# The down projection's split weights: low parts on the vector engine, buffers shared with the activations

## The chip, the cores and the metric

One core of one Trainium2 chip. A core has five engines that run their own queues of instructions: TensorE (PE in the profile: matmuls into PSUM; PEld: its loads of the stationary operand), the vector engine (DVE), the scalar engine (ACT), GpSimd (POOL) and SyncE (SP), which here issues all DMA transfers. The metric is the device time of one execution in microseconds (us).

## The reference

One layer of a decoder trunk on an input of 1024 rows (tokens) of 1024 float32 values: a mixer (recurrent heads and a causal convolution), a residual sum with a norm, and a gated feed-forward part with a second residual sum. The part that matters here is the feed-forward part:

```python
D_MODEL, SEQ, D_FF = 1024, 1024, 2816
def _conv_ffn(h, ffn_up, ffn_conv_w, ffn_conv_b, ffn_down):
    hid = h @ ffn_up                                     # 1024 x 5632
    hid = _causal_dwconv(hid, ffn_conv_w, ffn_conv_b)    # width 3
    gate, up = hid[..., :D_FF], hid[..., D_FF:]
    return (jax.nn.gelu(gate, approximate=True) * up) @ ffn_down   # the down projection
...
x = x + _rms_norm(f, norm_post_ffn)                      # f: its result
```

All of it is float32.

## The kernel before

**Split operands.** A float32 matmul is made of three matmuls on a faster format (float32r): an operand is split into a high part (a cast, on ACT) and a low part (the operand minus its high part), and high x high, high x low and low x high are added up in PSUM. `split` (L153) issues both: the cast on ACT, and the subtraction on POOL or DVE. `weight` (L158) loads a weight tile of 128x512 (256 KB) with a DMA on SP into a raw buffer (tag `wr`, three of them) and splits it into `wh` and `wl` (two buffers of each). Its low part is made on POOL unless the weight is a held one. Activations are split too, with the low part on DVE, into pairs of tiles called `a`, from the pool `h1p`, which has 16 tiles (8 pairs).

**The down projection** (`ffn_down`, L947) multiplies a 1024 x 2816 matrix by a 2816 x 1024 one in quarters, with seven products instead of eight (the Strassen-Winograd scheme). The rows fall in two halves, 0 and 1, and the inner dimension in two halves of 11 tiles of 128 (`HT` = 11): `A11`, `A12` are lists of 11 activation tiles of half 0, `A21`, `A22` of half 1. The weights' combinations (`T(n)`) were added up earlier, by `weight_sums`, and lie in DRAM (`sums`). The other three products read `ffn_down` itself (`B(r, c)`). The activations' combinations are made during the products:

- product 1 (`A11`) and 3 (`A12`) add up in the four banks `X`, product 2 (`A11 - A21`, tiles `s`) and 4 (`A22`) in the banks `Y`, product 5 (`A22`) in `X`, product 6 (`A11`) in `Y`, product 7 (`A12`) in `X`;
- while product 4 runs, `after4` adds `A21` to `A22`; with product 5, `after5` turns `A11` into `A22 - A11`; with product 6, `after6` turns `A12` into `A12 - A11`. These are 33 additions of 128x512 on DVE (line 959 in the profile; the tiles are called `act` or `row` by the pool that they lie in). Each may run as soon as its operands are ready, also ahead of its product.

`product` (L965) goes through the 11 tiles j: it splits the activation tile, calls `then(j)` (the additions), loads and splits the weight, and issues 12 matmuls, three for each of four row tiles t. At the end it calls `after(t)` for each row tile.

**Held weights.** Seven weights of product 7 are loaded and split ahead, during products 5 and 6 (`hold`): raw in `f2p` (six buffers, which also serve the pieces of the input in the last step), high and low part in `hp`, the 16 tiles in which `A21` and five tiles of `A22` lie until they are used up. Their low parts are made on DVE. The matmuls of held weights come last and in the order of t, so that the four row tiles end one after the other and the norm and output of one go on beside the matmuls of the next (`last`, `second`, `norm`, `ffn_out`).

**Order.** The instructions' order on each engine is set before the run by a scheduler that works with priorities and estimated times: `high_priority` puts a block ahead of everything without it, and within that the program's order decides among what is ready. On the chip each engine works its queue in that order and waits where an operand or a buffer isn't ready.

Of the kernel before, what the change touches and what calls it, by code (L numbers as in the profile page):

```python
# [12 lines left out]
F32 = mybir.dt.float32  # L13
F32R = mybir.dt.float32r
# [7 lines left out]
P = 128  # L22
# [16 lines left out]
HT = FT // 2  # L39
# [2 lines left out]
LN_EPS = 1e-5  # L42
GN_EPS = 64e-5

HELD = 7
DECAY = math.exp(-0.5)


# [46 lines left out]
class Trunk:  # L95
    def __init__(self, ctx, tc, a):
        self.ctx, self.tc, self.nc, self.a = ctx, tc, tc.nc, a
        self.at = dict(PRIO)
        self.n = 0


    def nm(self, s):
# [28 lines left out]
    def after(self, i, first):  # L131

        self.tc.add_manual_dep(
            i.ins, first.ins.name,
            mybir.DependencyInfo(mybir.DependencyClass.NoSync, mybir.DependencyReason.DATA),
            reason="the bank's first matmul clears it")
# [18 lines left out]
        eng = self.nc.gpsimd if pool else self.nc.vector  # L155
        return self.nc.scalar.copy(hi, src), eng.tensor_tensor(lo, src, hi.bitcast(F32), ALU.subtract)  # L156

    def weight(self, src, shape, home=None, held=False):  # L158

        with self.tc.high_priority():  # L160
            raw = (self.f2p.tile(shape, F32, tag="f2", name=self.nm("wr")) if held else
                   self.wp.tile(shape, F32, tag="wr", bufs=3, name=self.nm("wr")))
            self.nc.sync.dma_start(raw, src)
            if held:
                hi, lo = (self.hp.tile(shape, F32R, tag="h", name=self.nm("w")) for _ in range(2))
            elif home:
                hi, lo = (home[0].tile(shape, F32R, tag=t, bufs=BUFS[t], name=self.nm("wm")) for t in home[1:])
            else:
                hi, lo = (self.wp.tile(shape, F32R, tag=t, bufs=2, name=self.nm(t)) for t in ("wh", "wl"))
            self.low = self.split(hi, lo, raw, not held)[1]  # L170
        return hi, lo


# [773 lines left out]
    def ffn_down(self, acts):  # L947
        nc = self.nc
        first = self.tc.high_priority
        A11, A12, A21, A22 = acts[0][:HT], acts[0][HT:], acts[1][:HT], acts[1][HT:]  # L950
        B = lambda r, c: lambda j: self.a["ffn_down"][c, r * HT + j]
        T = lambda n: lambda j: self.sums[n - 1, j]
        X = [self.bank() for _ in range(4)]
        Y = [self.bank(("pb", "pn")[t // 2]) for t in range(4)]
        halves = lambda: [row[:, c * 512:(c + 1) * 512] for row in (self.row("nrow", 4) for _ in range(2)) for c in range(2)]
        four = lambda: [self.tp.tile([P, 512], F32, tag="tp", name=self.nm("c")) for _ in range(4)]

        def tt(out, a, b, op=ALU.add):
            nc.vector.tensor_tensor(out, a, b, op)  # L959
            return out  # L960

        def s3(j):
            return tt(self.f2p.tile([P, HALF], F32, tag="f2", name=self.nm("s3")), A11[j], A21[j], ALU.subtract)

        def product(banks, src, wt, start, after, then=lambda j: None, held=(), soon=True):  # L965
            ops, n = [], HT - len(held)
            for j in range(HT):
                with first():
                    hi, lo = self.pair("a", self.h1p)
                    self.split(hi, lo, src(j))  # L970
                    then(j)
                wh, wl = self.weight(wt(j), [P, 512]) if j < n else held[j - n]
                op = (hi, wh), (hi, wl), (lo, wh)
                if j >= n:
                    ops.append(op)
                else:
                    for t in range(4):
                        mms(banks[t], t, op, start and j == 0, j == HT - 1)

            ins = []  # L980
            for t in range(4):
                for i, op in enumerate(ops):
                    ins += mms(banks[t], t, op, False, i == len(held) - 1)
                with first() if soon else ExitStack():
                    after(t)
            self.chain(ins)

        def mms(ps, t, op, start, stop):
            return [self.mm(ps, a[:, t * P:(t + 1) * P], w, start=start and i == 0, stop=stop and i == 2, skip=True)
                    for i, (a, w) in enumerate(op)]  # L990

        def norm(h, t, c, f, src, junk):
            nc.scalar.activation(junk, src, AF.Square, accum_out=self.fss[:, 4 * h + t, c:c + 1])  # L993
            tt(f, src, self.post_ffn[:, c * 512:(c + 1) * 512], ALU.mult)

        s1, s7 = halves(), halves()
        product(X, lambda j: A11[j], B(0, 0), True, lambda t: nc.scalar.copy(s1[t], X[t]))
        product(Y, s3, T(3), True, lambda t: nc.scalar.copy(s7[t], Y[t]))
        c11 = four()
        product(X, lambda j: A12[j], B(1, 0), False, lambda t: norm(  # L1000
            0, t, 0, c11[t], X[t], self.f2p.tile([P, 512], F32, tag="f2", name=self.nm("junk"))))
        c21 = four()
        late = []

        def hold(j, every=2):

            if j % every == 1 and len(late) < HELD:
                late.append(self.weight(B(1, 1)(HT - HELD + len(late)), [P, 512], held=True))


        def after4(j):
            tt(A22[j], A21[j], A22[j])

        def after5(j):
            hold(j, 3)
            tt(A11[j], A22[j], A11[j], ALU.subtract)

        def after6(j):
            hold(j)
            tt(A12[j], A12[j], A11[j], ALU.subtract)  # L1020

        product(Y, lambda j: A22[j], T(4), False, lambda t: tt(c21[t], s1[t], Y[t]), after4)
        product(X, lambda j: A22[j], T(1), True, lambda t: tt(s7[t], s7[t], X[t]), after5)

        def second(t):
            tt(c21[t], c21[t], Y[t])
            tt(s1[t], s1[t], Y[t])
            norm(1, t, 0, c21[t], c21[t], Y[t])
            tt(s7[t], s7[t], s1[t])
            norm(1, t, 1, s7[t], s7[t], Y[t])  # L1030
            self.ffn_out(4 + t, (c21[t], s7[t]))

        def last(t):
            tt(s1[t], s1[t], X[t])
            norm(0, t, 1, s1[t], s1[t], X[t])
            self.ffn_out(t, (c11[t], s1[t]))

        product(Y, lambda j: A11[j], T(2), True, second, after6, soon=False)
        product(X, lambda j: A12[j], B(1, 1), False, last, held=late)
# [258 lines left out]
```

## Time and profile before

| | |
|---|---|
| median of 3 runs | 1340.19 us (1337.7 to 1342.9) |
| the profiled execution | 1338.02 us, of it 1336.2 us from the first to the last instruction (the span) |
| mean granted TensorE clock | 0.982 |
| busy share of the span | PE 95%, DVE 64%, ACT 51%, POOL 46% |
| matmuls of the down projection | from 1089.3 us to 1325.6 us of the span |

A row of the groups gives line, engine, operation, output<-inputs, shapes and count, then busy time in us and the mean of one in ns, then the idle time of the engine just ahead of these instructions and what ended it. A row of the waits gives the waiting engine with its tile and line, the one it waited for, the us in all, the number of times, and the longest. A row of the timeline gives the start in us, the length in us, the engine and the instruction, xN for N merged ones, and in brackets the idle time before it.

### The profile page before, as it was taken

The page shows a single profiled execution, that of the slowest core. Times are in us where ns is not written, and L with a number is a line of the kernel's source. Part 1 is how long each engine was busy: PE and PEld are TensorE (multiplying, and loading weights), DVE is VectorE, ACT ScalarE, POOL GpSimd, SP SyncE. Part 2 cuts the span into 40 slices and gives each one's busy share as a digit, 9 for nine tenths or more (in the row PEclk, how much of TensorE's full clock was granted, in tenths as well). Part 3 has the DMA queues.
Part 4 walks back from the last instruction along what each step waited for, and adds up shares of the span by engine and source line. Part 5 has one row for each costly group of instructions (what it writes and reads, how often), then busy time and mean ns, then how long its engine had stood idle before and what let it go on. Part 6 is the DMA issues. An engine that isn't in the chain of part 4 may idle for free. (4 is left out here: it accounts for less than half of the span.)

```text
span 1336.2 us, 22956 instructions
## 1 busy us (share of the span) xinstructions
PE 1266.3 (95%) x8580; PEld 1019.7 (76%) x8580; DVE 860.7 (64%) x1450; ACT 679.6 (51%) x1354; POOL 618.8 (46%) x522
## 2 busy tenths in 40 slices
PE   6999989999899989999999999999999989996996
PEld 5767767777678767787798788888888878875885
DVE  5377998997799989885521463455555365295347
ACT  6563654657755765656543564333333344443451
POOL 4343423354333322444462467667676454445441
PEclk9999979999999999999999999999999999997998
DMA  6322211222123441222355655665654323343325
GB/s 213 79 77 62 72 40 49 52 69 56 50 66 104 149 144 50 64 72 79 103 162 172 234 197 179 199 191 178 197 177 139 95 79 95 95 122 123 95 80 204
DMA packets 85647, 155.79 MB, mean 117 GB/s; under 512 B 9280, under 2 KB 15808, under 8 KB 85536
## 3 DMA queue, kind: packets, MB, share of 16 engines
q1 hardware_dynamic: 85536, 154.33, 38.1%
q8 instruction: 67, 1.10, 0.4%
q14 instruction: 44, 0.36, 0.1%
HBM read 129.13 MB, written 25.17 MB: 115 GB/s over the span
## 5 line engine op out<-in xcount | busy, mean ns | idle before, releaser
L156 POOL TENSOR_TENSOR wl<-wr,wh 128x512 fp32r<-128x512 f32 x350 | 474.9, 1358 | 548.9 <-ACT wh L156 522.2
L129 PE MATMUL pb<-f,wh 128*128 128x512 f32 x1408 | 442.3, 395 | 3.2 <-ACT pb L771 1.8
L156 ACT CAST wh<-wr 128x512 fp32r<-128x512 f32 x350 | 215.1, 615 | 326.5 <-PE pb L129 167.4
L129 PEld LDWEIGHTS pb<-f,wh 128*128 128x128 f32 x1408 | 263.7, 188 | 61.9 <-ACT pb L771 2.0
L129 PE MATMUL pb<-f,wl 128*128 128x512 f32 x704 | 280.1, 398 | 2.0 <-POOL wl L156 2.0
L129 PE MATMUL pb<-h,wh 128*128 128x512 f32 (+3 forms) x720 | 229.8, 399 | 2.5 <-ACT wh L156 1.9
L877 DVE SCALAR_TENSOR_TENSOR acc<-pb,params,acc 128x511 f32<-128x511 f32 (+1 forms) x128 | 95.5, 746 | 183.8 <-ACT acc L872 123.9
L399 DVE SCALAR_TENSOR_TENSOR pc<-c,params,pc 128x512 f32<-128x512 f32 x232 | 174.2, 751 | 4.6 <-ACT pc L396 0.5
L129 PEld LDWEIGHTS pb<-f,wl 128*128 128x128 f32 x704 | 132.6, 188 | 35.7 <-POOL wl L156 5.4
L129 PEld LDWEIGHTS pb<-h,wh 128*128 128x128 f32 (+2 forms) x720 | 132.3, 189 | 34.4 <-ACT wh L156 4.3
L129 PE MATMUL pb<-h,wl 128*128 128x512 f32 (+3 forms) x360 | 146.7, 408 | 3.0 <-POOL wl L156 2.8
L129 PE MATMUL pb<-wh,a 128*128 128x512 f32 x428 | 141.9, 400 | 3.4 <-ACT wh L156 3.4
L129 PEld LDWEIGHTS pb<-wh,a 128*128 128x128 f32 x428 | 81.4, 191 | 23.8 <-ACT wh L156 4.3
L129 PE MATMUL pb<-wl,a 128*128 128x512 f32 x214 | 86.7, 405 | 11.3 <-POOL wl L156 11.3
L129 PEld LDWEIGHTS pb<-h,wl 128*128 128x128 f32 (+2 forms) x360 | 68.1, 189 | 22.3 <-POOL wl L156 5.8
L156 DVE TENSOR_TENSOR a<-act,a 128x512 fp32r<-128x512 f32 x50 | 37.3, 746 | 66.1 <-ACT a L156 66.1
L156 ACT CAST a<-act 128x512 fp32r<-128x512 f32 x50 | 31.0, 621 | 71.7 <-PE pn L129 47.5
L129 PEld LDWEIGHTS pb<-wl,a 128*128 128x128 f32 x214 | 41.1, 192 | 23.1 <-POOL wl L156 13.3
L877 DVE SCALAR_TENSOR_TENSOR pt<-pb,params,pt 128x511 f32<-128x511 f32 (+1 forms) x48 | 35.8, 746 | 33.7 <-ACT ecarry L874 33.1
L917 POOL TENSOR_TENSOR b<-b,b 128x512 f32<-128x512 f32 x44 | 57.0, 1295 | 0.9
L872 ACT ACTIVATE acc<-pb,params 128x512 f32<-128x512 f32 x64 | 49.5, 774 | 1.8 <-PE pb L129 1.8
L129 PE MATMUL pn<-wh,a 128*128 128x512 f32 x132 | 47.8, 403 | 0.0
(297 smaller groups left out, 1928.3 us busy)
## 6 DMA issues: line engine op xcount, KB each, us to landing
wr<-ffn_up SPq DMA_DIRECT2D x176, 256.0 KB, 2.7
wr<-w_in SPq DMA_DIRECT2D x80, 256.0 KB, 2.6
b<-ffn_down SPq DMA_DIRECT2D x44, 256.0 KB, 4.0
sums<-b SPq DMA_DIRECT2D x44, 256.0 KB, 2.4
wr<-sums SPq DMA_DIRECT2D x44, 256.0 KB, 2.6
wr<-ffn_down SPq DMA_DIRECT2D x33, 256.0 KB, 2.6
wr<-w_out SPq DMA_DIRECT2D x32, 256.0 KB, 2.7
mixd<-t SPq DMA_DIRECT2D x16, 256.0 KB, 3.2
```

The source lines that it names most:

```text
L129: return self.nc.tensor.matmul(out, lhsT, rhs, start=start, stop=stop, skip_group_check=skip)
L156: return self.nc.scalar.copy(hi, src), eng.tensor_tensor(lo, src, hi.bitcast(F32), ALU.subtract)
L399: nc.vector.scalar_tensor_tensor(out, c[:, j:j + HALF], w(j), acc, ALU.mult, ALU.add)
L872: nc.scalar.activation(acc, ps, AF.Identity, scale=w(2), bias=self.par("fb", ch))
L877: nc.vector.scalar_tensor_tensor(acc[:, o:], ps[:, :HALF - o], w(j), acc[:, o:], ALU.mult, ALU.add)
L917: sub = lambda o, x, y, op=ALU.subtract: nc.gpsimd.tensor_tensor(o, x, y, op)
```

## The change

In the down projection, the low part of every weight is made on DVE (`low_pool` turns False as `ffn_down` begins; the earlier stages keep POOL). Weights of odd j that aren't held take their high and low tiles from the 16 tiles of `h1p`, in turn with the activations' pairs; those of even j keep `wh` and `wl`. Both load into the three raw buffers. Five weights of product 7 are held instead of seven, so six of its weights are streamed.

```diff
-HELD = 7
+HELD = 5
...
+        self.low_pool = True
...
-    def weight(self, src, shape, home=None, held=False):
+    def weight(self, src, shape, home=None, held=None):
 
         with self.tc.high_priority():
-            raw = (self.f2p.tile(shape, F32, tag="f2", name=self.nm("wr")) if held else
+            raw = (self.f2p.tile(shape, F32, tag="f2", name=self.nm("wr")) if held is self.hp else
                    self.wp.tile(shape, F32, tag="wr", bufs=3, name=self.nm("wr")))
             self.nc.sync.dma_start(raw, src)
             if held:
-                hi, lo = (self.hp.tile(shape, F32R, tag="h", name=self.nm("w")) for _ in range(2))
+                hi, lo = self.pair("w", held)
             elif home:
...
-            self.low = self.split(hi, lo, raw, not held)[1]
+            self.low = self.split(hi, lo, raw, self.low_pool)[1]
...
     def ffn_down(self, acts):
         nc = self.nc
         first = self.tc.high_priority
+        self.low_pool = False
...
-                wh, wl = self.weight(wt(j), [P, 512]) if j < n else held[j - n]
+                wh, wl = self.weight(wt(j), [P, 512], held=self.h1p if j % 2 else None) if j < n else held[j - n]
...
-                late.append(self.weight(B(1, 1)(HT - HELD + len(late)), [P, 512], held=True))
+                late.append(self.weight(B(1, 1)(HT - HELD + len(late)), [P, 512], held=self.hp))
```

## The prediction

> **What bounds the kernel now.** I read the page first, then the busy times by stretch over the last 280 us (the down projection), then what TensorE (PE) waited for there, and last the instructions in order of time at the two places where it waited.
>
> ```profile
> span 1336.2 us, 22956 instructions
> PE 1266.3 (95%) x8580; PEld 1019.7 (76%) x8580; DVE 860.7 (64%) x1450; ACT 679.6 (51%) x1354; POOL 618.8 (46%) x522
> ...
> L156 POOL TENSOR_TENSOR wl<-wr,wh 128x512 fp32r<-128x512 f32 x350 | 474.9, 1358 | 548.9 <-ACT wh L156 522.2
> ...
> L156 ACT CAST wh<-wr 128x512 fp32r<-128x512 f32 x350 | 215.1, 615 | 326.5 <-PE pb L129 167.4
> ```
>
> PE is busy 95% of the span, so what a change off PE can win is PE's holes. The down projection's columns by stretch are length, then busy time and count for PE, PEld, DVE, ACT and POOL, then the granted PE clock:
>
> ```profile
> 1085.00:1100.00 15.00, 11.51 (x44) 8.91 (x43) 12.40 (x19) 7.71 (x15) 10.42 (x4) 0.89 0.20 57
> ...
> 1125.00:1156.00 31.00, 31.00 (x134) 24.95 (x134) 7.63 (x11) 14.70 (x28) 14.21 (x11) 1.00 0.33 94
> 1156.00:1187.00 31.00, 31.00 (x135) 24.95 (x134) 21.62 (x22) 14.71 (x29) 15.10 (x11) 1.00 0.33 94
> 1187.00:1220.00 33.00, 21.74 (x78) 15.68 (x77) 27.37 (x41) 12.52 (x25) 16.91 (x7) 0.79 0.48 151
> ...
> 1233.00:1264.00 31.00, 31.00 (x134) 24.98 (x133) 11.35 (x17) 12.76 (x23) 14.21 (x11) 1.00 0.35 94
> ```
>
> PE is full in three of the five stretches. It has 3.5 us of hole in 1085 to 1100 and 11.3 us in 1187 to 1220, and the clock is lower in just these two. How much that is in all comes from the matmuls of the seven products, from the first to the last:
>
> ```profile
> 1089.33 1.09 PE L129 MATMUL pb<-wh,a 128*128 128x512 f32 x4
> ...
> L129 PE MATMUL pb<-wh,a 128*128 128x512 f32 x428 | 141.9, 400 | 3.4 <-ACT wh L156 3.4
> L129 PE MATMUL pb<-wl,a 128*128 128x512 f32 x214 | 86.7, 405 | 11.3 <-POOL wl L156 11.3
> L129 PE MATMUL pn<-wh,a 128*128 128x512 f32 x132 | 47.8, 403 | 0.0
> L129 PE MATMUL pn<-wl,a 128*128 128x512 f32 x66 | 26.6, 403 | 0.0
> ...
> 1305.82 19.76 PE L129 MATMUL pb<-w,a 128*128 128x512 f32 x84
> ```
>
> 428 + 214 + 132 + 66 + 84 = 924 matmuls (7 products x 11 weights x 12). The last 84 run without a hole: (19.76 - 0.40) / 83 = 0.2333 us each, and 2.80 us a weight. 924 of them need 215.6 us. They took 1325.58 - 1089.33 - 0.16 (the last one's overlap) = 236.1 us. So **20.5 us** are lost: 5.1 at the first place (15 - 11.51 = 3.5 idle, and 0.11 x 15 = 1.6 by the clock), and the other 15.4 around the second.
>
> Who is late there, first place and then second, with POOL's instructions at both:
>
> ```profile
> PE pb L129 <- POOL wl L156: 3.5, 1, 3.5
> ...
> PE pb L129 <- POOL wl L156: 7.8, 3, 7.5
> ACT w L156 <- DVE act L959: 6.0, 1, 6.0
> PE pb L129 <- ACT wh L156: 3.4, 2, 3.0
> ...
> 1087.23 8.39 POOL L156 TENSOR_TENSOR wl<-wr,wh 128x512 fp32r<-128x512 f32 x2 [1.50 <-PE pb L129]
> ...
> 1193.51 1.29 POOL L156 TENSOR_TENSOR wl<-wr,wh 128x512 fp32r<-128x512 f32 x1 [2.60 <-ACT wh L156]
> ...
> 1205.64 10.21 POOL L156 TENSOR_TENSOR wl<-wr,wh 128x512 fp32r<-128x512 f32 x2 [5.93 <-ACT wh L156]
> ```
>
> A weight's low part takes POOL 1.29 us; two together took 8.39 and 10.21 us, 5.8 and 7.6 too many. What DVE did meanwhile, from 1205.6 to 1213.4:
>
> ```profile
> L959 DVE TENSOR_TENSOR act<-act,act 128x512 f32<-128x512 f32 x8 | 5.2, 685 | 0.0
> L156 DVE TENSOR_TENSOR a<-act,a 128x512 fp32r<-128x512 f32 x3 | 2.1, 685 | 0.0
> L156 DVE TENSOR_TENSOR w<-wr,w 128x512 fp32r<-128x512 f32 x2 | 1.4, 686 | 0.0
> L959 DVE TENSOR_TENSOR act<-act,row 128x512 f32<-128x512 f32 x1 | 0.7, 684 | 0.0
> ```
>
> Fourteen instructions with two operands in SBUF each, at full pace (0.69 us), idle 0.0: while DVE runs such a chain, POOL's instruction stands still. The other 3.4 us come through ACT: its cast of a held weight waited 6.0 us for DVE, and PE's next weight was queued behind it. The reverse shows too, over 1156 to 1220:
>
> ```profile
> L959 DVE TENSOR_TENSOR act<-act,act 128x512 f32<-128x512 f32 x17 | 14.6, 871 | 0.1
> L156 DVE TENSOR_TENSOR a<-act,a 128x512 fp32r<-128x512 f32 x18 | 13.4, 747 | 15.7 <-ACT a L156 15.7
> L959 DVE TENSOR_TENSOR row<-act,row 128x512 f32<-128x512 f32 x8 | 9.5, 1186 | 0.2
> L959 DVE TENSOR_TENSOR act<-act,row 128x512 f32<-128x512 f32 x8 | 7.4, 920 | 0.0
> L156 DVE TENSOR_TENSOR w<-wr,w 128x512 fp32r<-128x512 f32 x7 | 5.9, 850 | 0.3 <-ACT w L156 0.3
> L959 DVE TENSOR_TENSOR c<-pb,post_ffn 128x512 f32<-128x512 f32 x4 | 2.6, 677 | 0.0
> ```
>
> 62 instructions, 53.4 us; at 0.685 they would be 42.5. So about 10.9 us of DVE time went to instructions that POOL held up.
>
> **The change, part by part.**
>
> *Low parts to DVE.* 70 streamed weights change engine, 1.29 us on POOL for 0.69 on DVE. The waits of PE for POOL (3.5 and 7.8) go, and with them the lowered clock behind them. DVE pays 11 x 0.69 = 7.6 us a product. Where PE is full it has room: 7.6 + 7.6 = 15.2 of 31 us in 1125 to 1156, 11.4 + 7.6 = 19.0 of 31 in 1233 to 1264. In 1156 to 1187 it is 21.6 + 7.6 = 29.2 of 31, before what the end of the sharing gives back. Over 1156 to 1220 POOL made 11 + 7 = 18 low parts: + 12.3 us on DVE, - 10.9 us for the sharing, - 1.4 us for two held weights fewer, so + 0.0. DVE's load at its fullest place stays as it is. The additions of the later products that fill it may run late there: they are wanted one or two products on, 31 us each.
>
> [...]
>
> *Odd weights in the activations' 16 buffers.* Before, a weight's buffer came free when PE had done the weight two before it: one weight's time, 2.80 us, for a cast (0.62) and POOL's 1.29. Now even weights have the two pairs for themselves, so the buffer is free three weights ahead (8.4 us) for 0.62 + 0.69. The eight shared pairs serve 1.5 pairs a weight instead of 1: 5.3 weights ahead, 14.9 us, where it was 8. Each split needs 1.3 us of that. Cost zero; were the ring's order bad, rival 3 prices it. The transfers stay 77 x 256 KB and in the program's order; the three raw buffers come free after a low part as before, 0.6 us earlier each.
>
> *Five held weights, not seven.* Two weights of the last product go from the quarter-by-quarter part to the streamed part. PE's 924 matmuls are the same. In the crowded place two casts, two low parts and two transfers fewer stand in line: good for ACT's 3.4 us wait, but that wait hangs on the buffers that DVE's additions free. I bound what is left of the second place from 0 to 3.4 us, beside the case in which all of it stays (rival 1), and take 1.5, near half of the largest wait, 3.0, since DVE's load there is unchanged while POOL no longer upsets the order.
>
> *The tail.* After product six DVE works through sums and squares to the first output:
>
> ```profile
> 1293.42 0.69 DVE L959 TENSOR_TENSOR c<-c,pb 128x512 f32<-128x512 f32 x1 [0.28 <-PE pb L129]
> ...
> L959 DVE TENSOR_TENSOR nrow<-nrow,nrow 128x512 f32<-128x512 f32 x4 | 3.8, 958 | 0.0
> L959 DVE TENSOR_TENSOR c<-c,post_ffn 128x512 f32<-128x512 f32 x4 | 3.7, 954 | 0.0
> ...
> 1311.13 0.75 DVE L944 SCALAR_TENSOR_TENSOR x<-c,ss,x 128x512 f32<-128x512 f32 x1 [0.60 <-POOL ss L151]
> ...
> 1332.35 0.75 DVE L944 SCALAR_TENSOR_TENSOR x<-nrow,ss,x 128x512 f32<-128x512 f32 x1 [0.16 <-DMA x<-x1d]
> ```
>
> From 1311.13 on, sixteen pieces go through six buffers (load, add, store), 21.2 us to the last, and PE's end at 1325.6 lies inside that. Into the stretch before 1311.13 come at most six low parts of the last product, 6 x 0.69 = 4.1 us; out of it goes what POOL's last instructions cost, 8 x 0.27 = 2.2 us. With some three of the six made ahead it is even. Quarters that end 15 x 0.233 = 3.5 us apart, where it was 21 x 0.233 = 4.9, still end before their buffers come. I take 0, between - 2.2 and + 1.9.
>
> **Sum.** The profiled execution's own time is 1338.0 (span 1336.2 and 1.8 around it), 2.2 below the median of the three runs, 1340.2. 1338.0 - 20.5 + 1.5 + 0 = 1319.0; from the median it would be 1321.2. I forecast **1320**. With the bounds, 1338.0 - 20.5 - 2.2 = 1315.3 to 1340.2 - 20.5 + 3.4 + 1.9 = 1325: the likeliest case's own range is 1315 to 1325.
>
> **The rivals.**
>
> 1. *DVE takes POOL's place at the crowded spot.* Its low parts stand in one queue with 33 additions and the held weights. For it: DVE's 27.4 of 33 us, and ACT's 6.0 us wait behind DVE. Against: low parts are issued ahead of later products' additions, and are made some three weights ahead. If all 15.4 us stay there, only the first place is won: 1338.0 - 5.1 = 1333. Chance 0.11.
>
> 2. *The long low parts are not due to DVE's chain*, but to something of the weight itself (its buffer, its place in line) that goes along to DVE. For it: only two of 70 are long, and DVE is in a chain at other times too. Against: fourteen DVE instructions without a gap all through the longer one. Then PE's 3.5 and 7.5 us stay, and the clock's 1.6 and up to 15.4 - 11.3 = 4.1: 1338.0 - 20.5 + 16.7 = 1334. Chance 0.04. [...]
>
> 3. *Slower: the shared ring.* If an odd weight got its pair only as PE finished the weight before, each of the 33 odd streamed weights (six products x 5, and 3) would come a cast and a low part late: 33 x (0.62 + 0.69) = 43 us, less the 20.5: 1361. It decides from 20.5 / 33 = 0.62 us per odd weight on; to be slower by 0.5% takes 0.9. For it: the buffers are given out in one order, and DVE's queue holds all behind a late cast. Against: 14.9 us of lead for 1.3 us of work. Chance 0.05. [...]
>
> **Numbers.** The likeliest case has 0.80. Half a percent of this time, 6.7 us, is about what a measurement can tell, so "faster" ends at 1333.5. Rivals 1 and 2 lie at that edge; half of their 0.15 counts as faster, half as same. Faster 0.87, same 0.08, slower 0.05. The range for 8 in 10 holds the likeliest case and most of rivals 1 and 2: 1314 to 1334.
>
> **What the profile after would show.** Right: no low part of a `ffn_down` weight on POOL; DVE's sums in the crowded place at 0.69 us; products 30.8 us apart with PE full and the clock at 1.00; about 216 to 218 us from the first to the last matmul, and 10.6 us behind it. Wrong: PE waiting for DVE's low part in the fourth product (rival 1), a hole of about 1.3 us at each odd weight (rival 3), or a first output more than 2 us later against PE's end.

## The result, and the profile after

The changed kernel takes 1319.78 us in the median (1318.51 to 1322.45, 4 runs) where the kernel before takes 1340.41: a ratio of 0.985, 95% interval 0.983 to 0.987. The profiled execution took 1319.54 us. The forecast was 1320.

The changed kernel's page:

```profile
span 1317.8 us, 22852 instructions
PE 1259.8 (96%) x8580; PEld 1015.9 (77%) x8580; DVE 877.9 (67%) x1520; ACT 680.0 (52%) x1354; POOL 515.3 (39%) x452
```

Its busy times in the stretches that were shown of the kernel before (the columns are the same):

```profile
1085.00:1100.00 15.00, 15.00 (x66) 12.09 (x65) 14.11 (x27) 10.39 (x20) 1.30 (x1) 1.00 0.43 124
...
1125.00:1156.00 31.00, 31.00 (x135) 25.05 (x134) 14.64 (x23) 14.60 (x26) 0.00 (x0) 1.00 0.31 97
1156.00:1187.00 31.00, 31.00 (x135) 25.09 (x134) 23.15 (x38) 15.36 (x32) 0.00 (x0) 1.00 0.39 121
1187.00:1220.00 33.00, 33.00 (x143) 26.69 (x143) 32.73 (x55) 15.23 (x28) 0.00 (x0) 1.00 0.51 153
...
1233.00:1264.00 31.00, 31.00 (x135) 25.05 (x135) 16.86 (x27) 12.88 (x23) 0.00 (x0) 1.00 0.30 94
```

PE is full in all five stretches and its clock is 1.00 in each. POOL is empty after the last weight of the stage before. DVE is busy 32.73 of 33 us at the crowded place, and PE doesn't wait for it. Where the time went is read from the timeline: the first and last matmuls of the seven products, and then the first and last piece of the final sum:

```profile
1090.17 1.10 PE L131 MATMUL pb<-wh,a 128*128 128x512 f32 x4
...
1299.75 5.30 PE L131 MATMUL pb<-w,a 128*128 128x512 f32 x22
```

```profile
1291.49 0.75 DVE L946 SCALAR_TENSOR_TENSOR x<-c,ss,x 128x512 f32<-128x512 f32 x1 [0.38 <-POOL ss L153]
1313.87 0.75 DVE L946 SCALAR_TENSOR_TENSOR x<-nrow,ss,x 128x512 f32<-128x512 f32 x1 [1.01 <-DMA x<-x1d]
```

The products take 1305.05 - 0.16 - 1090.17 = 214.7 us where they took 236.1: 21.4 us less. The tail behind the last matmul is 1317.8 - 1305.05 = 12.75 us where it was 1336.2 - 1325.58 = 10.62: 2.1 more. The products begin 0.8 us later. 21.4 less 2.1 and 0.8 is, but for rounding, the 18.4 us by which the span is shorter.

### The profile page after: what moved, and what is told of

Its sections match the earlier page's. It is cut to its first block, busy times and chain, and to the rows that moved or that the text cites. A ratio compares the mean times of both kernels' runs of the same rounds, so it can differ in the third digit from the quotient of the medians.

```text
span 1317.8 us, 22852 instructions
## 1 busy us (share of the span) xinstructions
PE 1259.8 (96%) x8580; PEld 1015.9 (77%) x8580; DVE 877.9 (67%) x1520; ACT 680.0 (52%) x1354; POOL 515.3 (39%) x452
## 4 chain that ended last, share of the span: by engine, by line
PE 72%; DVE 15%; ACT 4%; DMA 3%; issue 3%; POOL 2%; SPq 1%; POOLq 0%; ACTq 0%; DVEq 0%
PE pb L131 60%; DVE pc L401 4%; PE pe L131 4%; PE pn L131 3%; PE xs L131 3%; POOL wl L158 1%; DVE dw L578 1%; DMA x<-x1d 1%; ACT wh L158 1%; DVE pt L470 1%; DVE nrow L962 1%; DMA wr<-ffn_up 1%; PE pe L146 1%; DVE kk L471 1%; DVE h L265 1%
## 5 line engine op out<-in xcount | busy, mean ns | idle before, releaser
L158 POOL TENSOR_TENSOR wl<-wr,wh 128x512 fp32r<-128x512 f32 (+1 forms) x280 | 369.9, 1322 | 439.6 <-ACT wh L158 413.1
L158 ACT CAST wh<-wr 128x512 fp32r<-128x512 f32 (+1 forms) x319 | 195.9, 615 | 331.1 <-PE pb L131 171.8
L153 POOL TENSOR_TENSOR ss<-var,mhalf 128x1 f32<-128x1 f32 x16 | 11.0, 694 | 230.1 <-DVE ss L943 203.3
L131 PE MATMUL pb<-w,a 128*128 128x512 f32 x366 | 89.8, 393 | 0.0
L131 PE MATMUL pb<-wh,a 128*128 128x512 f32 x240 | 81.5, 396 | 0.0
L131 PEld LDWEIGHTS pb<-w,a 128*128 128x128 f32 x366 | 68.7, 188 | 16.1
L131 PEld LDWEIGHTS pb<-wh,a 128*128 128x128 f32 x240 | 45.1, 188 | 10.6
L131 PE MATMUL pb<-wl,a 128*128 128x512 f32 x120 | 47.7, 397 | 0.0
L158 DVE TENSOR_TENSOR a<-act,a 128x512 fp32r<-128x512 f32 x50 | 33.3, 687 | 18.4 <-ACT a L158 18.3
```

Of the source, the lines that this page charges most:

```text
L131: return self.nc.tensor.matmul(out, lhsT, rhs, start=start, stop=stop, skip_group_check=skip)
```

## The experiments

Three theories at first. A: POOL's low parts stand still while DVE runs an unbroken chain of instructions with two operands in SBUF, so the change of engine pays. B: the lead that the shared ring gives to odd weights pays. C: the held weights' casts, which block ACT, made the second place.

**The engine alone.** On the changed kernel:

```diff
-HELD = 5
+HELD = 7
-  ... held=self.h1p if j % 2 else None) if j < n
+  ... held=None) if j < n
```

> Only the low parts move to DVE; seven held weights and the two-deep wh and wl buffers stay as before. Theory A (POOL's low parts stood still while DVE ran chains, so the engine is what pays): both long waits go, the ACT wait of 3.4 us behind a held weight may stay; 1318 to 1325 us. Theory B (what pays is lead: odd weights in the shared ring are made further ahead): the holes of both places stay with two-deep buffers, now as waits for DVE; 1331 to 1338 us.

Measured: 1329.01 us (ratio 0.993, 0.990 to 0.995), half of the gain, in neither theory's range (A 1318 to 1325, B 1331 to 1338). What PE waited for in the products, and then the busy times at the crowded place:

```profile
PE pb L131 <- DVE wl L158: 5.8, 7, 1.9
```

```profile
1187.00:1220.00 33.00, 29.84 (x125) 22.56 (x124) 28.76 (x49) 15.48 (x28) 0.00 (x0) 1.00 0.52 160
```

The long waits are gone (the longest is 1.9 us), and seven short ones for DVE have come: with buffers two deep a low part has one weight's time (2.80 us), and DVE's queue holds it up longer than that. The products took 225.4 us by the trace, so 9.8 of the 20.5 lost us stayed: 4.4 in the fourth product, 4.5 in the last one. With the shared ring and the same seven held weights the kernel takes 1318.74 us (below), so the other half of the gain is the ring's.

**The ring alone**, with five held weights, the streamed weights' low parts back on POOL:

```diff
-        self.low_pool = False
...
-            self.low = self.split(hi, lo, raw, self.low_pool)[1]
+            self.low = self.split(hi, lo, raw, held is not self.hp)[1]
```

> The shared ring and five held weights, but the streamed weights' low parts stay on POOL. Theory A: POOL's long instructions (7 to 9 us) stay; at the start of the first product there is no lead, so 5 us are lost there, and at the crowded place a lead of 8.4 us hides a part; 1326 to 1336 us, with instructions of over 5 us on POOL still in the trace. Theory B: the lead hides all, 1318 to 1322 us.

Measured: 1331.56 us (0.995, 0.993 to 0.997). From the timeline POOL's longest instruction, from the waits PE's longest, and the busy times at the first place:

```profile
1203.18 10.87 POOL L158 TENSOR_TENSOR w<-wr,w 128x512 fp32r<-128x512 f32 x1 [5.86 <-PE pn L131]
```

```profile
PEld pb L131 <- POOL wl L158: 9.6, 1, 9.6
```

```profile
1085.00:1100.00 15.00, 15.00 (x66) 12.10 (x65) 12.82 (x13) 10.65 (x19) 10.65 (x8) 1.00 0.45 131
```

Theory A's range, but not all of its story: the lead clears the first place (PE full), which A had down as lost. At the crowded place one low part takes 10.87 us, and PE waits 9.6 us for the one behind it in POOL's queue. Neither part alone does it; the two gains, 10 and 7.5 us, add up to 17.5 of the 20. In the length of the products alone they are 10.7 and 10.0 us (225.4 and 226.1 instead of 236.1) of 21.4, so each part cures losses that the other leaves.

**Five held weights alone.** The kernel before with

```diff
-HELD = 7
+HELD = 5
```

> The kernel before with five held weights instead of seven, nothing else. Theory A: both long POOL instructions stay, at most the ACT wait of 3.4 us and its clock go; 1334 to 1341 us. Theory C (held weights' casts that block ACT are what made the second place): the second place's 15 us go, 1323 to 1326 us.

Measured: 1341.84 us (1.001, 1.000 to 1.003): nothing, and a little above theory A's range. Both long instructions of POOL are there, and theory C falls as it was put, since the second place's 15 us stay. ACT's wait of 6.0 us behind DVE is still there with five held weights, so what that wait costs isn't settled by this run:

```profile
1090.17 8.39 POOL L156 TENSOR_TENSOR wl<-wr,wh 128x512 fp32r<-128x512 f32 x2 [1.50 <-PE pb L129]
1208.65 9.61 POOL L156 TENSOR_TENSOR wl<-wr,wh 128x512 fp32r<-128x512 f32 x2 [5.93 <-ACT wh L156]
```

**The additions without priority**, on the kernel before, which was to break DVE's chain and leave POOL its work:

```diff
                 with first():
                     hi, lo = self.pair("a", self.h1p)
                     self.split(hi, lo, src(j))
-                    then(j)
                 ... (weight and matmuls)
+                then(j)
```

> The kernel before (low parts on POOL, seven held, two-deep buffers), with the 33 additions of products 4 to 6 issued without priority, so that DVE's chain at the crowded place is broken up or moved. Theory A: where the chain goes, the 9 us POOL instruction goes too, and the first place (5 us) stays: 1323 to 1330 us if the additions find room elsewhere. If the long low part is due to something of the weight itself, it stays: 1336 to 1342 us.

Measured: 1340.53 us (1.001, 1.000 to 1.003). It doesn't tell the theories apart, for the chain stayed: DVE is busy 27.8 of 33 us at the crowded place, where it was 27.4, and the long instruction is as long as before:

```profile
1207.01 10.21 POOL L156 TENSOR_TENSOR wl<-wr,wh 128x512 fp32r<-128x512 f32 x2 [4.73 <-ACT wh L156]
```

**Breaks in the chain, and their control.** Both are the kernel before with one short instruction more on DVE behind each of the 33 additions, here of `after4`. The first reads one operand, the second two:

```diff
             tt(A22[j], A21[j], A22[j])
+            nc.vector.tensor_reduce(self.spot, A22[j][:, 0:128], AX.X, ALU.add)      # breaks
+            tt(self.spot, A22[j][:, 0:128], self.post_ffn[:, 0:128])                 # control
```

> The kernel before (low parts on POOL) with one short instruction more on DVE behind each of the 33 additions: a sum over 128 columns, one operand in SBUF, some 0.2 us, its result unused. Theory A (an unbroken chain of instructions with two operands in SBUF keeps POOL out): POOL gets in at these breaks, no low part takes over 3.5 us at the crowded place, and of the 15 us there at least 6 go: 1326 to 1335 us; the first place has none of them and keeps its 7 us instruction. If POOL's long instruction is due to something else: 9 us stay, 1338 to 1346 us.

> The control of the run with breaks: the kernel before, with a short addition of 128 columns and two operands in SBUF behind each of the 33 additions, results unused. Theory A: no break for POOL, so a low part of 9 us or more stays at the crowded place: 1338 to 1348 us. If the other run gains only because DVE's order is shifted, this one gains as much: 1326 to 1335 us.

Measured: with breaks 1329.66 us (0.995, 0.993 to 0.996), the control 1340.05 us (1.001, 0.999 to 1.003). POOL's low parts from 1160 to 1225 (shortest, median and longest in ns), and the group of the added instruction; first with breaks, then the control:

```profile
L156 POOL TENSOR_TENSOR wl<-wr,wh x21: 1277/1462/1815, 1159.9 to 1224.6; 128x512 fp32r<-128x512 f32 x21
```

```profile
L1014 DVE TENSOR_REDUCE spot<-act 128x1 f32<-128x128 f32 x11 | 3.0, 276 | 0.0
```

```profile
L156 POOL TENSOR_TENSOR wl<-wr,wh x19: 1270/1297/9593, 1159.2 to 1222.9; 128x512 fp32r<-128x512 f32 x19
```

```profile
L960 DVE TENSOR_TENSOR spot<-act,post_ffn 128x128 f32<-128x128 f32 x10 | 5.0, 502 | 0.0
```

This settles the cause of the second place's long low part and of PE's wait for it. DVE has more to do in both, low parts stay on POOL, the weights' buffers are the same. An instruction of 0.28 us with one operand lets POOL in, the longest low part falls from 9.6 to 1.8 us, and PE's longest wait for POOL there from 8.5 to 0.7. The two added instructions also differ in kind and length; which of these opens the way isn't shown. The first place got no breaks and kept its 8.41 us pair.

The gain in time is not all due to that. The last matmuls of both runs, with breaks and then the control:

```profile
1303.61 19.39 PE L129 MATMUL pb<-w,a 128*128 128x512 f32 x84
```

```profile
1314.05 19.77 PE L129 MATMUL pb<-w,a 128*128 128x512 f32 x84
```

With breaks they start (19.39 - 0.40) / 83 = 0.2288 us apart, in the control 0.2333, and so it is all through the products. Of the 9.8 us by which the products are shorter than the control's (227.2 against 237.0), 924 x 0.0045 = 4.2 are these faster matmuls. The other 5.6 are what the breaks won, a little under the 6 expected. What stayed lost is 227.2 - 924 x 0.2288 = 15.8 us: 5.4 at the first place, and about 10.3 at the second, where the control loses 16.1. There PE stands still for 5.3 us (longest 2.7 us, behind ACT), and most of the rest goes by the granted clock: it was 0.90 from 1187 to 1220, by an estimate 0.10 x 33 = 3.3 us.

**POOL's work back, with nothing hanging on it.** The changed kernel with, for each streamed weight,

```diff
+            tick = self.tickp.tile([P, 1], F32, tag="tick", bufs=40, name=self.nm("tick"))
+            with first():
+                nc.scalar.copy(tick, hi[:, 0:1].bitcast(F32))
+                i = nc.gpsimd.tensor_tensor(self.tock, tick, tick, ALU.add)
+                with self.tc.issue_after(i.ins):
+                    nc.gpsimd.tensor_tensor(self.scr, self.post_ffn[:, :512], self.post_ffn[:, 512:], ALU.subtract)
```

> The changed kernel with one subtraction of 128x512 on POOL per streamed weight, released by the weight's cast, its result unused and nothing waiting for it. Theory A: POOL's instructions take over 5 us in DVE's chain at the crowded place although no weight hangs on them, and DVE's take up to 1.7 us. If DVE has no time to spare there (busy 32.7 of 33 us), some 12 x 1.0 us for POOL come back as waits of PE: 1325 to 1332 us; if its order leaves the additions to slip, 1319 to 1322 us.

Measured: 1340.41 us (1.001, 1.000 to 1.003): all of the gain is lost again, more than either expectation. The longest of POOL's instructions, then PE's waits, then a group of DVE's from 1187 to 1220:

```profile
1212.95 15.90 POOL L961 TENSOR_TENSOR tock<-tick 128x1 f32<-128x1 f32 x1 [3.97 <-ACT tick L960]
```

```profile
PE pb L131 <- DVE wl L158: 10.0, 7, 2.1
PE pb L131 <- DVE a L158: 3.1, 3, 1.3
```

```profile
L158 DVE TENSOR_TENSOR wl<-wr,wh 128x512 fp32r<-128x512 f32 x5 | 6.1, 1214 | 0.0
```

An addition of one column took POOL 15.9 us while DVE was in its chain, and a DVE low part grew from 0.69 to 1.21 us in the mean. The small additions (0.19 us where undisturbed) are part of that traffic, and ACT made one copy more for each weight, so this is a bound on what POOL's work costs here and not its price alone. It shows how little DVE has to spare.

**The tail.** Four runs together, the changed kernel again and three variants of it. What each edits:

```diff
-HELD = 5
+HELD = 7                                  # seven held
...
+        self.low_pool = True              # last product's low parts on POOL
         product(X, lambda j: A12[j], B(1, 1), False, last, held=late)
...
-        xs = [self.f2p.tile(... tag="f2" ...) ...]
+        pool, tag = (self.f2p, "f2") if tt > 3 else (self.hp, "h")        # pieces in hp
+        xs = [pool.tile(... tag=tag ...) ...]
```

> The changed kernel again, as the reference for the three beside it: 1318 to 1322 us by every theory, with a tail of about 12.9 us behind the last matmul.

> The changed kernel with seven held weights. Theory A: PE stays full (two more casts and low parts in the crowded place, where DVE is busy 32.7 of 33 us without PE waiting); the quarters end 4.9 us apart instead of 3.5, four low parts instead of six fall into the last product, so the tail is 1 to 2 us shorter: 1318 to 1320 us. If the crowded place is at its limit, ACT's wait behind a held weight comes back: 1322 to 1330 us.

> The changed kernel with the six streamed low parts of product 7 on POOL. If the tail's extra 2 us come from the six low parts on DVE, the first output is up to 4 us earlier against the last matmul, less 1 us for each DVE instruction that POOL holds up: 1317 to 1320 us. If DVE's chain of sums there starves POOL as it did elsewhere, PE waits for a low part of 3 to 9 us in product 7: 1323 to 1330 us.

> The changed kernel with the last eight of the sixteen pieces of the final sum loaded into free tiles of hp instead of the six buffers of f2p. If those six buffers' round of load, sum and store sets the tail, the last piece is ready some 5 us behind the last matmul and the tail falls from 12.9 to about 9 us: 1315 to 1317 us. If DVE's queue or the transfers themselves set it, no change: 1319 to 1321 us.

| | median us (ratio to before, 95%) | products begin | products take | tail |
|---|---|---|---|---|
| changed kernel | 1318.92 (0.984 to 0.987) | 1090.0 | 214.7 | 12.5 |
| seven held | 1318.74 (0.983 to 0.986) | 1092.5 | 214.8 | 10.5 |
| last low parts on POOL | 1324.70 (0.986 to 0.990) | 1096.5 | 214.7 | 12.1 |
| pieces in hp | 1317.32 (0.983 to 0.986) | 1088.7 | 214.7 | 10.7 |

(Begin, length and tail are from each profile; the tail counts from 0.2333 us after the last matmul's start.) PE stays full in all, also with two held weights more, as expected there. The tail's extra 2 us go with seven held weights and stay with the low parts on POOL: the number held makes them, not DVE's six low parts. The kernel before with five held weights agrees (13.1 us against 10.8 with seven), but each tail is that of one profile, and with breaks it was 12.1 with seven held. The pieces in hp shorten it to 10.7, not to the 9 expected. The medians of the first, second and fourth can't be told apart, so the tail's 2 us don't show in them: the products begin anywhere from 1088.7 to 1096.7 us in the profiles of all runs. The third's median is higher, as if PE waited in product 7, but neither PE's work nor the tail is longer. Its products began 6 us later, and PE is already 7 us late some 420 us into the span, where the program's order on PE is still the same; the profiles of the breaks and of their control are late by as much at that point. Two of its five runs took 1319.4 and 1319.6 us, as the changed kernel does. So its higher median says nothing on the low parts; why the earlier part is longer in some executions stays open.

**Both remedies for the tail**: seven held weights, and ten of the sixteen pieces in tiles of used activations:

```diff
-HELD = 5
+HELD = 7
...
+        pool, tag = (self.f2p, "f2") if 3 < tt < 7 else (self.ap, "act")
```

> The changed kernel with seven held weights, and with ten of the sixteen pieces of the final sum loaded into free activation tiles instead of the six buffers of f2p. If the round through six buffers sets the tail, the tail behind the last matmul falls to 9 us (10.5 with seven held weights alone, 10.7 with the pieces alone): 1314 to 1317 us. If DVE's queue sets it, it stays at 10.5: 1317 to 1320 us.

Measured: 1315.12 us (0.982, 0.981 to 0.984), the fastest of all, faster than both kernels in the median (the changed kernel's 1318.92 was measured beside another set of runs, and the intervals just touch). The tail is 8.3 us, below the 9 expected if the round through six buffers sets it. The last matmuls and the last piece:

```profile
1299.62 7.63 PE L131 MATMUL pb<-w,a 128*128 128x512 f32 x32
...
1311.44 0.74 DVE L947 SCALAR_TENSOR_TENSOR x<-nrow,ss,x 128x512 f32<-128x512 f32 x1
```

## Why the prediction was right, and where its steps were not

*The 20.5 us.* Right in size: 21.4 us went. The 0.9 beyond it is no wait. In the kernels with the shared ring, matmuls on a weight that lies in it follow each other a little faster. In the changed kernel twelve of them are

```profile
1098.56 2.92 PE L131 MATMUL pb<-w,a 128*128 128x512 f32 x12
...
1104.13 2.92 PE L131 MATMUL pb<-w,a 128*128 128x512 f32 x12
```

(2.92 - 0.39) / 11 = 0.230 us each, against 0.2333 for held weights. Two such groups start 5.57 us apart, with an even weight between them, where two weights took 5.60 before; over 33 such pairs that is about 1 us. The ring is not what it takes: the run with breaks has none and went at 0.2288.

*To whom they are due.* Here the step failed though the sum came out. The prediction gave all of the gain to the engine and put the ring at "cost zero". The engine alone leaves 9.8 us, the ring alone 9.6 at one place. The prediction had worked out the lead (2.80 us before, 8.4 to 14.9 after) and used it only against rival 3. That a low part on DVE with 2.80 us of lead is late behind DVE's own additions is what the run of the engine alone showed (seven waits, up to 1.9 us).

*The cause.* Rival 2 is refuted at the second place: with breaks in DVE's chain the long low part goes (1.8 us at the longest), with the control it stays (9.6). No run broke the chain at the first place, so there the same cause is argued. At the second place POOL was kept out over a chain and not for one instruction of 0.69 us: the control's longest low part took 9.6 us, its shortest 1.27. Three of DVE's additions in the changed kernel read

```profile
1210.54 1.90 DVE L962 TENSOR_TENSOR act<-act,act 128x512 f32<-128x512 f32 x3
```

so they start (1.90 - 0.69) / 2 = 0.60 us apart and last 0.69: each starts before the one ahead has ended. Whether it is this that keeps POOL out isn't shown.

*DVE's load, "+ 0.0".* The groups at the crowded place:

```profile
L158 DVE TENSOR_TENSOR a<-act,a 128x512 fp32r<-128x512 f32 x12 | 7.9, 689 | 0.0
L962 DVE TENSOR_TENSOR act<-act,act 128x512 f32<-128x512 f32 x12 | 7.8, 690 | 0.0
L158 DVE TENSOR_TENSOR w<-wr,w 128x512 fp32r<-128x512 f32 x11 | 7.4, 690 | 0.3 <-ACT w L158 0.3
```

The price of 0.69 us was right, and so was the end of the sharing: from 1156 to 1220 these three groups have means of 0.69 us, where they had 0.75 to 0.87 before. The load was put too low: 32.7 of 33 us are used, since without holes more weights pass in the same time (143 matmuls where it was 78). Rival 1 still didn't come about, because of the lead: the run of the engine alone, without it, still lost 9.8 us, with 5.8 us of waits of this kind.

*What is left of the second place, 1.5 us.* It was 0.

*The tail, 0, between - 2.2 and + 1.9.* It was + 2.1 in the first profile and + 1.6 in the second (12.5 against 10.8, counted as in the table). The term that was mis-sized is the held weights' one: "Quarters that end 15 x 0.233 = 3.5 us apart, where it was 21 x 0.233 = 4.9, still end before their buffers come". Low parts were named as the risk and aren't it. The first piece of the final sum starts 13.6 us ahead of PE's end (1305.05 - 1291.49) where it was 14.5, so 0.9 of the 2.1 are there already, and the round of the pieces takes the other 1.2 (22.4 instead of 21.2 us). That the total came out within 1 us is in part luck, since the errors cancel: 0.9 more won, 1.5 not lost, 2.1 lost in the tail.

*Rival 3.* No sign of it: in the changed kernel's products PE's waits are none.

## What to carry to other kernels

Where POOL and DVE both run elementwise instructions on SBUF, look at the longest instruction of POOL, not its mean: here the mean of a low part was 1.36 us, while two of them took 10.21 us under a stretch in which DVE was busy without a gap, and PE's longest wait for POOL there was 7.5 us. Moving the work to DVE alone won half here, since its results then stood in line behind DVE's other work (seven waits of PE, up to 1.9 us); together with the ring's lead and the same held weights it won all of it (1318.74 us). And when a sum of parts comes out, run the parts alone before you believe their shares, and look at the pace of the matmuls too before you book a gain as a wait that went.

## What was not expected of the hardware

A single DVE instruction of 0.28 us with one operand in SBUF, put between additions, brought POOL's longest low part down from 9.6 to 1.8 us. Even a POOL addition on one column was held for 15.9 us by a chain. And matmuls of the same size ran at 0.230 us with a weight in the shared ring and at 0.2288, with no such ring, in the run with breaks, against 0.2333 in the kernel before and in the control: 1.4 and 1.9% less. The run with breaks adds a tile of one column to the constants and its control, at 0.2333, one of 128 columns, so the place of the buffers may do it; that wasn't tried.
